# A streaming encoder step: factors of the norms spread by transposes, sums of the first norm taken from a token-major copy of x on ScalarE, first norm made beside the last units of an FFN

## The chip, the core and the metric

The kernel runs on one core of one Trainium2 chip. The core has TensorE (PE in the profile; PEld is its weight load), VectorE (DVE), ScalarE (ACT), GpSimd (POOL) and SyncE (SP), which issues most transfers; 16 DMA engines move the data. The metric is device time in microseconds (us). The kernel before takes 2417.05 us, the median of three runs (2413.43 to 2418.78).

## What is computed

One layer over 2048 prompt tokens and 8 x 16 sample tokens, width 1024, all in fp32. The layer normalizes x, projects it, runs four mixers side by side (a state-space scan, windowed attention, a short convolution, a convolution with layer norm), projects back, adds, and then runs a SwiGLU FFN of width 2816; a last norm ends it.

```python
def rms_norm(x, g):
    xf = x.astype(jnp.float32)
    y = xf * lax.rsqrt(jnp.mean(xf * xf, axis=-1, keepdims=True) + EPS)
    return (y * g.astype(jnp.float32)).astype(x.dtype)
...
    u = rms_norm(x, norm_mix) @ w_in
...
    mix = jnp.concatenate([ya, yb.astype(x.dtype), yc, yd], axis=-1)
    x = x + mix @ w_out
    hf = rms_norm(x, norm_ffn)
    x = x + (jax.nn.silu(hf @ w_gate) * (hf @ w_up)) @ w_down
...
    y_prompt = rms_norm(xp, norm_final)
    y_sample = rms_norm(xs, norm_final)
```

## The kernel before

**Tiling.** Everything is kept feature-major: 128 features on the partitions, tokens along the free axis, eight tiles deep for the width of 1024. The tokens are cut into five chunks c0 to c4 of 256, 512, 512, 512 and 384 tokens (c3 holds three prompt tiles and the 128 sample tokens). A matrix product is made in three passes: weights and activations are split into a high and a low part (`split`, `split_w`: a copy on ScalarE and a difference on VectorE), and `group` (L235) issues high x high (L239), high x low (L240) and low x high (L241) for each of the eight depth tiles. A unit, one weight tile of 128 output features, is 24 such matmuls.

**Weights.** `load_w` loads a raw tile (`fr`, two buffers) by SyncE's queue, ScalarE writes the high part (L204) and VectorE the low part (L184) into a `w` tile (three buffers). Some split tiles are stored to DRAM (`kept`) and loaded again for later chunks.

**Stages.** `weave` puts a list of units in order and runs steps of other work (tokens of generators) after given units. For c0 and c1 the program is: `proj_out(c)` (8 units), `proj_in(next)` (21 units, or what is left of them) with `norm2(c)` beside it, `ffn(c)` (44 gate and up units and 24 down units, the last six being the last gate, the last up and four downs that also square the result for the final norm) with the mixers of the next chunk beside it. c2 to c4 are woven differently: the FFN of c2 beside `proj_in` of c3 and c4, and the FFN of c3 and c4 together at the end, in an arithmetic of seven products (`quad`, L1129).

**The norms.** Each has three steps. Sums: squares on ScalarE, added up over the eight depth tiles on VectorE (`add_square`, into `ns`). Factors: `rstd_of` takes the sum over the partitions with one matmul by a column of ones per 128 tokens (L265), and `newton` makes the inverse root with ten small VectorE instructions. Spread: `spread` puts the factors of 128 tokens on all partitions by a matmul of the broadcast column with the identity (L272), into a PSUM tile `px`; then VectorE multiplies each depth tile by weight and factor and the tile is split into `act` tiles (16 buffers). `spread` serves the norm ahead of the mixers (`norm1`), the norm ahead of the FFN (`norm2`), the final norm and the end of two mixers (`end_ssd`, `end_conf`): 17 + 10 + 10 + 17 + 17 = 71 tiles of 128 tokens. The last two chunks use `spread_one` (L1046) for the norms behind their mixers.

**The first norm of c1 to c4** loads x twice by SyncE's queue: eight depth tiles for the sums (`norm1_stats`, L326) and eight for the scaling (`norm1`, L334), all through the three `nt` buffers. c0 keeps x in `act` tiles and is not touched by the change but for `spread`. The steps of `norm1(c2)` stand beside `proj_out(c1)` and those of `norm1(c3)` beside `proj_out(c2)` (L1000, L1006).

**Order.** A scheduler in the framework orders instructions by priority and by when it thinks that buffers come free. Weight loads have a higher priority. Each engine then runs its own list strictly in order, and SyncE's queue too; a matmul is bound to a place behind the last unit by `run` (L953).

Of the kernel before, what the change touches and what calls it, by code (L numbers as in the profile page):

```python
# [13 lines left out]
ALU = mybir.AluOpType  # L14
# [3 lines left out]
P = 128  # L18
# [97 lines left out]


@with_exitstack
def stream_step(ctx: ExitStack, tc: tile.TileContext, cfg, x, w_in, w_out, w_gu, w_down, tab, con, dist_p, dist_s,
                h0, xst, sst, gst, kc, vc, y, o_ssm_p, o_ssm_s, o_xc_p, o_xc_s, o_k_p, o_k_s, o_v_p, o_v_s,  # L120
                o_s_p, o_s_s, o_g_p, o_g_s):
    nc = tc.nc
# [20 lines left out]
    def mk(pool_, shape, tag, dt=F32, **kw):  # L143
        uid[0] += 1
        return pool_.tile(shape, dt, tag=tag, name=f"{tag}_{uid[0]}", **kw)
# [48 lines left out]
    def bc(a, shape):  # L194
        return a.to_broadcast(shape)
# [73 lines left out]
    def spread(r, T):  # L269
        pr = mk(px, [P, 512], "px")  # L270
        for b in range(T // P):
            pe.matmul(pr[:, b * P:(b + 1) * P], bc(r[:, b:b + 1], [P, P]), ident, start=True, stop=True)  # L272
        return pr[:, :T]

    def add_square(ss, src, T, first, eng=dve):
# [25 lines left out]

    def norm1_stats(c):
        T, o = c["T"], c["off"]
        ss = mk(np_, [P, TM], "ns", bufs=1)[:, :T]
        hold = c["i"] == 0 and KT * T <= 4 * TM
        if hold:

            c["x"] = []
            sq = []
            with tc.high_priority(offset=8 * AHEAD):  # L310
                xs = [mk(ap, [P, 2, KT // 4, T], "act") for _ in range(2)]
                for j in range(4):
                    sync.dma_start(xs[j // 2][:, j % 2], x[:, 2 * j:2 * j + 2, o:o + T])
                    c["x"] += [xs[j // 2][:, j % 2, k] for k in range(KT // 4)]
                qs = [mk(ap, [P, 2, KT // 4, T], "act") for _ in range(2)]
                for j in range(4):
                    sq.append(qs[j // 2][:, j % 2])
                    act.activation(sq[j], xs[j // 2][:, j % 2], AF.Square)
                for q in sq[1:]:
                    tt(sq[0], sq[0], q, ALU.add)  # L320
                tt(ss, sq[0][:, 0], sq[0][:, 1], ALU.add)
            yield
            c["r1"] = rstd_of(ss, T, D)
            yield
            return
        for k in range(KT):  # L326
            xt = mk(np_, [P, TM], "nt", bufs=B["nt"])[:, :T]
            sync.dma_start(xt, x[:, k, o:o + T])
            add_square(ss, xt, T, k == 0, dve)
        yield  # L330
        c["r1"] = rstd_of(ss, T, D)
        yield

    def norm1(c):  # L334
# [615 lines left out]
        yield  # L950


    def run(token):  # L953
        if tail[0] is None:
            next(token)
        else:
            with tc.issue_after(tail[0]):
                next(token)
# [12 lines left out]
    def twice(g, n=2):  # L971
        return [g] * n
# [14 lines left out]
    for t in twice(norm1_stats(chunks[0])) + twice(norm1(chunks[0]), 4):  # L987
# [5 lines left out]
    m0 = mixers(c0, True)  # L993
    nb0 = c0["blocks"]

    weave(units, (twice(norm1_stats(c1)) + twice(norm1(c1), 4), 6, n - 1), (m0[:nb0], 10, 22),
          (m0[nb0:], 18, len(units) - 1))
    for c, nxt, after in ((c0, c1, c2), (c1, c2, c3)):
        i = c["i"]
        weave(proj_out(c), *([(twice(final(chunks[i - 1]), 5), 0, 8), (twice(norm1(nxt), 4), 1, 8)] if i else []))  # L1000
        weave(proj_in(nxt, W_IN_TILES[0 if i else EARLY:]), (twice(norm2(c), 5), 0, 7))
        units = ffn(c)
        weave(units, (mixers(nxt), 0, int(len(units) * 0.85)),
              (twice(norm1_stats(after)), int(len(units) * 0.3), len(units) // 2))

    weave(proj_out(c2), (twice(final(c1), 5), 0, 8), (twice(norm1(c3), 4), 1, 8))  # L1006
    f = ffn(c2)
    def beside(c, s, units, end):

# [6 lines left out]

    s3 = proj_in(c3, SPREAD)
    units = s3[:5] + merge(s3[5:], f[:24]) + f[24:36]
    weave(units, (twice(norm2(c2), 5), 0, 5), *beside(c3, s3, units, len(units) - 1), (twice(norm1_stats(c4)), 20, 35))
    s4 = proj_in(c4, SPREAD)  # L1020
    units = proj_out(c3) + f[36:39] + merge(s4, f[39:44]) + f[44:53]
    weave(units, ([stats2(c3)], 8, 9), (twice(norm1(c4), 4), 8, 11), *beside(c4, s4, units, len(units) - 1))
# [260 lines left out]
def layout(cfg, inputs):  # L1283

    a = {k: np.asarray(v) for k, v in inputs.items()}
    f = np.float32

    def fm(t):

        return t.reshape(t.shape[0], -1, P).transpose(2, 1, 0)  # L1290

    xp, xs = a["x_prompt"][0], a["x_sample"].reshape(NS, D)
    parts, p0 = [], 0
    for i, n in enumerate(cfg.chunks):
        parts.append(xp[p0:p0 + n * P])
        p0 += n * P
        if i == cfg.sample_in:
            parts.append(xs)
    x = fm(np.concatenate(parts, 0))


    o = dict(z=0, x=256, B=512, C=640, dt=768, q=772, k=1028, v=1156, b=1284, c=1540, h=1796, a=2052, g=2308)
    hd = np.arange(64)

    def pair(base, t):
        return np.concatenate([base + HEADS[2 * t] * 64 + hd, base + HEADS[2 * t + 1] * 64 + hd])

    cols = []
    for n in W_IN_TILES:
        if n in ("z0", "z1", "x0", "x1", "q0", "q1"):  # L1310
            cols.append(pair(o[n[0]], int(n[1])))
        elif n == "dt":
            cols.append(o["dt"] + np.repeat(np.array(HEADS), 32))
        elif n in ("B", "C", "k", "v"):
            cols.append(o[n] + np.arange(P))
        else:
            cols.append(o[n[0]] + int(n[1]) * P + np.arange(P))
    w_in = a["w_in"][0][:, np.concatenate(cols)].reshape(KT, P, len(cols), P).transpose(2, 1, 0, 3)

    rows = np.concatenate([pair(0, 0), pair(0, 1), pair(256, 0), pair(256, 1), np.arange(512, 1024)])  # L1320
    w_out = a["w_out"][0][rows].reshape(KT, P, KT, P).transpose(2, 1, 0, 3)
    nff = cfg.nff
    w_gu = np.stack([a[n][0].reshape(KT, P, nff, P).transpose(2, 1, 0, 3) for n in ("w_gate", "w_up")], 1)
    w_down = a["w_down"][0].reshape(nff, P, KT, P).transpose(1, 2, 0, 3)

    tab = np.zeros((P, NTAB), f)

    def put(name, v, j=0):
        v = v.reshape(P, -1)
        tab[:, TAB[name] + j:TAB[name] + j + v.shape[1]] = v  # L1330

    for n, s in (("gmix", a["norm_mix"][0]), ("gffn", a["norm_ffn"][0]), ("gfin", a["norm_final"])):
        put(n, s.reshape(KT, P).T)
    inner = [pair(0, 0), pair(0, 1), 256 + np.arange(P), 384 + np.arange(P)]
    for j in range(4):
        put("xw", a["ssm_conv_w"][0][:, inner[j]].T, 4 * j)
        put("xb", a["ssm_conv_b"][0][inner[j]], j)
    for j in range(2):
        s = slice(j * P, (j + 1) * P)
        put("cw", a["cconv_w"][0][:, s].T, 31 * j)  # L1340
        put("sw", a["sconv_w"][0][:, s].T, 3 * j)
        put("cb", a["cconv_b"][0][s], j)
        put("lng", a["cconv_ln_g"][0][s], j)
        put("lnb", a["cconv_ln_b"][0][s], j)
        put("dsk", np.repeat(a["ssm_d"][0][[HEADS[2 * j], HEADS[2 * j + 1]]], 64), j)
        put("sng", a["ssm_norm"][0][pair(0, j)], j)
    put("dtb", np.repeat(a["ssm_dt_bias"][0][list(HEADS)], 32))
    put("alog", np.repeat(a["ssm_a_log"][0][list(HEADS)], 32))
    sinks = a["swa_sinks"][0]
    put("sinkp", np.tile(sinks[None], (P, 1)))  # L1350
    grp = (np.arange(P) // DEC_T) % 2
    for sg in range(2):
        for kv in range(2):
            put("sinks", sinks[kv * 2 + grp], sg * 2 + kv)

    con, bp, bs = constants()
    h0 = a["state_ssm"][0][:, list(HEADS)].transpose(3, 0, 1, 2).reshape(P, DEC_B, 256)
    xst = np.stack([a["state_ssm_conv"][0][:, :, inner[j]].transpose(2, 0, 1) for j in range(4)])
    sst = a["state_sconv"][0].reshape(DEC_B, 2, 2, P).transpose(2, 3, 0, 1)
    gst = a["state_cconv"][0].reshape(DEC_B, 30, 2, P).transpose(2, 3, 0, 1)  # L1360
    kc = a["cache_swa_k"][0].reshape(DEC_B, P, P).transpose(2, 0, 1)
    vc = a["cache_swa_v"][0].reshape(DEC_B, P, P).transpose(1, 0, 2)
    arrays = dict(x=x, w_in=w_in, w_out=w_out, w_gu=w_gu, w_down=w_down, tab=tab, con=con, dist_p=bp, dist_s=bs,
                  h0=h0, xst=xst, sst=sst, gst=gst, kc=kc, vc=vc)
    arrays = {k: np.ascontiguousarray(v) for k, v in arrays.items()}
    outs = dict(y=(P, KT, cfg.tokens), o_ssm_p=(P, 256), o_ssm_s=(P, DEC_B, 256), o_xc_p=(4, P, 3),
                o_xc_s=(4, P, DEC_B, 3), o_k_p=(P, P), o_k_s=(P, P), o_v_p=(P, P), o_v_s=(P, P), o_s_p=(2, P, 2),
                o_s_s=(2, P, DEC_B, 2), o_g_p=(2, P, 30), o_g_s=(2, P, DEC_B, 30))
    return arrays, outs
# [45 lines left out]
```

## Time and profile before

| what | value |
|---|---|
| median of 3 runs | 2417.05 us (2413.43, 2417.05, 2418.78) |
| the profiled execution: time | 2424.89 us |
| its span, first to last instruction | 2422.8 us |
| mean granted TensorE clock | 0.988 |
| instructions | 32494 |
| moved by DMA | 417.37 MB, mean 172 GB/s |

The span is one execution under the profiler, 2.1 us shorter than its own device time, and that execution is 7.8 us (0.3%) longer than the median of the runs. Rows of the page that begin with an engine's name give its busy time and share; rows with a line number give a group of equal instructions, with the mean of one and the time for which the engine stood idle just before them. "Idle" of an engine that nobody waits for is no loss. Rows of a timeline give start, length, engine, line, operation, and in brackets how long the engine had been idle and for whom.

### The profile page before, as it was taken

The page shows a single profiled execution, that of the slowest core. Times are in us where ns is not written, and L with a number is a line of the kernel's source. Part 1 is how long each engine was busy: PE and PEld are TensorE (multiplying, and loading weights), DVE is VectorE, ACT ScalarE, POOL GpSimd, SP SyncE. Part 2 cuts the span into 40 slices and gives each one's busy share as a digit, 9 for nine tenths or more (in the row PEclk, how much of TensorE's full clock was granted, in tenths as well). Part 3 has the DMA queues.
Part 4 walks back from the last instruction along what each step waited for, and adds up shares of the span by engine and source line. Part 5 has one row for each costly group of instructions (what it writes and reads, how often), then busy time and mean ns, then how long its engine had stood idle before and what let it go on. Part 6 is the DMA issues. An engine that isn't in the chain of part 4 may idle for free.

```text
span 2422.8 us, 32494 instructions
## 1 busy us (share of the span) xinstructions
PE 2358.7 (97%) x12451; PEld 2049.9 (85%) x12451; DVE 1597.3 (66%) x3001; ACT 880.8 (36%) x1466; POOL 144.2 (6%) x266
## 2 busy tenths in 40 slices
PE   6999999999999999998999999999999999999997
PEld 6888999988888888886878788888879999999997
DVE  7997998776884445567573554675687667663324
ACT  5544555433333333333312222233344444442221
POOL 0000000000000000001010000000001000000000
PEclk9999999999999999998999999999999999999998
DMA  6546444577555554465544336653633332339653
GB/s 213 202 160 226 149 153 161 165 260 270 192 176 174 174 174 167 173 240 147 176 146 145 143 123 225 209 168 116 213 109 135 113 131 95 119 122 319 211 182 119
DMA packets 133467, 417.37 MB, mean 172 GB/s; under 512 B 12880, under 2 KB 50672, under 8 KB 116160
## 3 DMA queue, kind: packets, MB, share of 16 engines
q1 hardware_dynamic: 115536, 324.57, 40.6%
q0 software_dynamic: 17776, 90.73, 9.8%
q8 instruction: 98, 1.61, 0.3%
q14 instruction: 57, 0.47, 0.1%
HBM read 324.07 MB, written 91.18 MB: 171 GB/s over the span
## 4 chain that ended last, share of the span: by engine, by line
PE 81%; issue 6%; DVE 6%; DMA 5%; ACT 2%; POOL 0%; SPq 0%; DVEq 0%; ACTq 0%; POOLq 0%
PE pm L239 17%; PE pm L240 17%; PE pm L241 17%; PE pm L1124 7%; PE pm L1125 7%; PE pm L1126 7%; DVE w L184 2%; PE px L1125 1%; PE px L1124 1%; PE px L1126 1%; DMA nt<-x 1%; ACT w L204 1%; DMA fr<-w_in 1%; DMA o_xc_s<-raw 1%; DVE mix L187 1%
## 5 line engine op out<-in xcount | busy, mean ns | idle before, releaser
L239 PE MATMUL pm<-act,w 128*128 128x512 f32 (+2 forms) x2216 | 803.8, 363 | 9.2 <-ACT act L199 7.4
L240 PE MATMUL pm<-act,w 128*128 128x512 f32 (+2 forms) x2216 | 794.6, 359 | 7.4 <-DVE act L184 7.3
L241 PE MATMUL pm<-act,w 128*128 128x512 f32 (+2 forms) x2216 | 795.5, 359 | 3.4 <-DVE w L184 3.4
L204 ACT ACTIVATE w<-fr 128x1024 fp32r<-128x1024 f32 (+2 forms) x380 | 393.6, 1036 | 893.4 <-PE pm L241 513.0
L184 DVE TENSOR_TENSOR w<-fr,w 128x1024 fp32r<-128x1024 f32 (+2 forms) x380 | 454.3, 1196 | 280.8 <-ACT w L204 279.1
L239 PEld LDWEIGHTS pm<-act,w 128*128 128x128 f32 x2216 | 418.9, 189 | 73.7 <-ACT act L199 9.2
L240 PEld LDWEIGHTS pm<-act,w 128*128 128x128 f32 x2216 | 419.5, 189 | 65.2 <-DVE act L184 8.7
L241 PEld LDWEIGHTS pm<-act,w 128*128 128x128 f32 x2216 | 419.1, 189 | 63.6 <-DVE w L184 4.7
L1124 PE MATMUL pm<-hf,w 128*128 128x448 f32 x616 | 225.2, 366 | 0.0
L1125 PE MATMUL pm<-hf,w 128*128 128x448 f32 x616 | 224.8, 365 | 0.0
L1126 PE MATMUL pm<-hf,w 128*128 128x448 f32 x616 | 223.8, 363 | 0.0
L187 DVE SCALAR_TENSOR_TENSOR mix<-raw,tabh,mix 128x384 f32<-128x384 f32 (+3 forms) x360 | 203.2, 593 | 2.4
L239 PE MATMUL pm<-h,w 128*128 128x512 f32 (+1 forms) x528 | 191.8, 364 | 5.3 <-ACT hf L199 3.3
L241 PE MATMUL pm<-h,w 128*128 128x512 f32 (+1 forms) x528 | 188.0, 357 | 0.0
L240 PE MATMUL pm<-h,w 128*128 128x512 f32 (+1 forms) x528 | 188.0, 357 | 0.0
L187 DVE SCALAR_TENSOR_TENSOR ft<-ft,pm 128x512 f32<-128x512 f32 (+1 forms) x132 | 78.6, 595 | 106.5 <-PE pm L241 90.5
L184 DVE TENSOR_TENSOR x<-x,pm 128x512 f32<-128x512 f32 (+2 forms) x184 | 108.2, 600 | 59.1 <-PE pm L241 51.2
L1126 PEld LDWEIGHTS pm<-hf,w 128*128 128x128 f32 x616 | 115.7, 188 | 9.4
L1124 PEld LDWEIGHTS pm<-hf,w 128*128 128x128 f32 x616 | 115.6, 188 | 9.4 <-ACT g L1138 0.3
L1125 PEld LDWEIGHTS pm<-hf,w 128*128 128x128 f32 x616 | 115.7, 188 | 8.3
L239 PEld LDWEIGHTS pm<-h,w 128*128 128x128 f32 x528 | 100.0, 190 | 23.6 <-ACT hf L199 3.7
L241 PEld LDWEIGHTS pm<-h,w 128*128 128x128 f32 x528 | 99.8, 189 | 15.2
(286 smaller groups left out, 2585.5 us busy)
## 6 DMA issues: line engine op xcount, KB each, us to landing
w<-kept SPq DMA_DIRECT2D x83, 1024.0 KB, 4.9
fr<-w_gu SPq DMA_DIRECT2D x154, 512.0 KB, 3.3
kept<-w POOLq DMA_DIRECT2D x51, 1024.0 KB, 6.3
fr<-w_down SPq DMA_DIRECT2D x84, 512.0 KB, 3.6
fr<-w_in SPq DMA_DIRECT2D x52, 512.0 KB, 4.0
fr<-w_out SPq DMA_DIRECT2D x40, 512.0 KB, 3.2
hm<-h POOLq DMA_DIRECT2D x44, 448.0 KB, 4.3
ht<-hm SPq DMA_DIRECT2D x40, 448.0 KB, 4.7
```

The lines of the kernel that those rows point to most:

```text
L184: return eng.tensor_tensor(out=out, in0=a, in1=b, op=op)
L187: return eng.scalar_tensor_tensor(out=out, in0=a, scalar=s, in1=b, op0=op0, op1=op1)
L204: act.activation(d[:, 0, :n], raw, AF.Copy)
L239: pe.matmul(ps[:, :T], wh, o[:, 0, :T], start=(i == 0), stop=False)
L240: pe.matmul(ps[:, :T], wh, o[:, 1, :T], start=False, stop=False)
L241: mm = pe.matmul(ps[:, :T], wl, o[:, 0, :T], start=False, stop=(i == n - 1))
L1124: pe.matmul(ps[:, :N], wh[:, i], a, start=first and i == 0, stop=False, skip_group_check=True)
L1125: pe.matmul(ps[:, :N], wh[:, i], b, start=False, stop=False, skip_group_check=True)
L1126: mm = pe.matmul(ps[:, :N], wl[:, i], a, start=False, stop=(i == n - 1), skip_group_check=True)
```

## The change

There are three edits. `spread` calls `pe.transpose` with the same operands where it called `pe.matmul`. `norm1_stats` for c1 to c4 reads rows of a second, token-major copy of x (`xr`, laid out on the host): for each 128 tokens two loads of 128 x 512, each squared on ScalarE in place with the sum of the row taken along (`accum_out`), and one VectorE addition of the two sums. The sums then stand with tokens on the partitions, as `newton` wants them, so the matmuls by ones and the adding up of eight tiles go. And the four steps of `norm1(c2)` and `norm1(c3)` now come beside the last six units of `ffn(c0)` and `ffn(c1)`; `norm1(c4)` stays where it was.

```diff
     def spread(r, T):
         pr = mk(px, [P, 512], "px")
         for b in range(T // P):
-            pe.matmul(pr[:, b * P:(b + 1) * P], bc(r[:, b:b + 1], [P, P]), ident, start=True, stop=True)
+            pe.transpose(pr[:, b * P:(b + 1) * P], bc(r[:, b:b + 1], [P, P]), ident)
         return pr[:, :T]
...
-        for k in range(KT):
-            xt = mk(np_, [P, TM], "nt", bufs=B["nt"])[:, :T]
-            sync.dma_start(xt, x[:, k, o:o + T])
-            add_square(ss, xt, T, k == 0, dve)
-        yield
-        c["r1"] = rstd_of(ss, T, D)
+
+        nb = T // P
+        sums = mk(cp, [P, 8], "n8", bufs=9)[:, :nb]
+        for b in range(nb):
+            for h in range(2):
+                xt = mk(np_, [P, TM], "nt", bufs=B["nt"])
+                part = mk(cp, [P, 1], "n1", bufs=4) if h else sums[:, b:b + 1]
+                sync.dma_start(xt, xr[o + b * P:o + (b + 1) * P, h * 512:(h + 1) * 512])
+                act.activation(xt, xt, AF.Square, accum_out=part)
+                if h:
+                    tt(sums[:, b:b + 1], sums[:, b:b + 1], part, ALU.add)
+            if b % 2:
+                yield
+        if nb % 2:
+            yield
+        v, r, t = (mk(cp, [P, 8], "n8", bufs=9)[:, :nb] for _ in range(3))
+        newton(v, r, t, sums, D)
+        c["r1"] = r
         yield
...
-        weave(proj_out(c), *([(twice(final(chunks[i - 1]), 5), 0, 8), (twice(norm1(nxt), 4), 1, 8)] if i else []))
+        weave(proj_out(c), *([(twice(final(chunks[i - 1]), 5), 0, 8)] if i else []))
...
-              (twice(norm1_stats(after)), int(len(units) * 0.3), len(units) // 2))
+              (stats1(after), int(len(units) * 0.3), len(units) // 2),
+              (twice(norm1(after), 4), len(units) - 6, len(units)))
...
-    weave(proj_out(c2), (twice(final(c1), 5), 0, 8), (twice(norm1(c3), 4), 1, 8))
+    weave(proj_out(c2), (twice(final(c1), 5), 0, 8))
```

**TensorE, the spread of c2's factors.** Before, it stands in `proj_out(c1)` behind that of the final norm of c0 (`px_5482`); `pm_5453` and `pm_5513` are units of `proj_out(c1)`.

```order
L240 MATMUL pm_5453<-act_4899,w_5450 128x512
L241 MATMUL pm_5453<-act_4899,w_5450 128x512
L272 MATMUL px_5482<-con_85,n_843_5431 128x128 x2
L272 MATMUL px_5489<-con_85,n_615_3821 128x128 x4
L239 MATMUL pm_5513<-act_2562,w_5510 128x512
```

Now it stands between the last gate unit (`pm_5180`) and the last up unit (`pm_5230`) of `ffn(c0)`.

```order
L240 MATMUL pm_5180<-act_2377,w_5177 128x256
L241 MATMUL pm_5180<-act_2377,w_5177 128x256
L272 MATMUL px_5208<-con_85,n_619_3889 128x128 x4
L239 MATMUL pm_5230<-act_2188,w_5227 128x256
L240 MATMUL pm_5230<-act_2188,w_5227 128x256
```

The spread has moved ahead by five units; it is one row of four blocks in both programs.

**VectorE, the end of `ffn(c0)`.** Before, from the product with the last gate (`ft` by `pm_5202`) to the first sums of the last downs (`x` by `pm_5269`, `pm_5282`); `w` are weight splits for the downs, `h_5261` is the low part of the last FFN tile.

```order
L187 SCALAR_TENSOR_TENSOR ft_5227<-ft_5227,pm_5202 128x256
L184 TENSOR_TENSOR w_5298<-fr_5296,w_5298 128x768
L187 SCALAR_TENSOR_TENSOR ft_5227<-ft_5227,pm_5235 128x256
L184 TENSOR_TENSOR w_5331<-fr_5329,w_5331 128x768
L184 TENSOR_TENSOR h_5261<-ft_5227,h_5261 128x256
L184 TENSOR_TENSOR x_302_1826<-x_302_1826,pm_5269 128x256
L184 TENSOR_TENSOR x_306_1860<-x_306_1860,pm_5282 128x256
```

Now, from the product with the last gate (`pm_5180`) to the first sum (`pm_5276`); `nt` and `act` are tiles of `norm1(c2)`, 512 tokens wide.

```order
L187 SCALAR_TENSOR_TENSOR ft_5205<-ft_5205,pm_5180 128x256
L187 SCALAR_TENSOR_TENSOR nt_5213<-nt_5213,tab_84,px_5208 128x512
L184 TENSOR_TENSOR w_5305<-fr_5303,w_5305 128x768
L184 TENSOR_TENSOR act_5216<-nt_5213,act_5216 128x512
L187 SCALAR_TENSOR_TENSOR nt_5219<-nt_5219,tab_84,px_5208 128x512
L187 SCALAR_TENSOR_TENSOR ft_5205<-ft_5205,pm_5230 128x256
L187 SCALAR_TENSOR_TENSOR nt_5259<-nt_5259,tab_84,px_5208 128x512
L184 TENSOR_TENSOR w_5350<-fr_5348,w_5350 128x768
L184 TENSOR_TENSOR act_5222<-nt_5219,act_5222 128x512
L184 TENSOR_TENSOR h_5256<-ft_5205,h_5256 128x256
L184 TENSOR_TENSOR act_5262<-nt_5259,act_5262 128x512
```

Three scalings and three splits of `norm1(c2)` have come among these rows, five of them ahead of the low part `h`.

**SyncE's queue at the start.** Before, from the fifth w_in tile (`fr_351`) to the seventh (`fr_440`); `nt` are tiles for the sums of c1, `x` the tiles of x that `proj_out(c0)` adds to.

```order
L222 DMA fr_351<-w_in 128x1024
L328 DMA nt_492<-x 128x512
L855 DMA x_331_2040<-x 128x256
L855 DMA x_336_2076<-x 128x256
L328 DMA nt_497<-x 128x512
L222 DMA fr_407<-w_in 128x1024
L222 DMA fr_440<-w_in 128x1024
```

Now, from the same fifth tile to the sixth (`fr_407`); `nt` by L333 are rows of the token-major copy, `nt` by L355 the first tiles of `norm1(c1)`.

```order
L222 DMA fr_351<-w_in 128x1024
L333 DMA nt_567<-xr 128x512
L333 DMA nt_570<-xr 128x512
L355 DMA nt_787<-x 128x512
L867 DMA x_307_1885<-x 128x256
L867 DMA x_312_1921<-x 128x256
L867 DMA x_317_1957<-x 128x256
L355 DMA nt_793<-x 128x512
L355 DMA nt_886<-x 128x512
L867 DMA x_322_1993<-x 128x256
L867 DMA x_327_2029<-x 128x256
L222 DMA fr_407<-w_in 128x1024
```

The sixth weight tile now has ten loads between it and the fifth instead of four.

More of the change, by code (lines that the diff above doesn't have):

```diff
@@ L118, in stream_step @@
 @with_exitstack
-def stream_step(ctx: ExitStack, tc: tile.TileContext, cfg, x, w_in, w_out, w_gu, w_down, tab, con, dist_p, dist_s,
+def stream_step(ctx: ExitStack, tc: tile.TileContext, cfg, x, xr, w_in, w_out, w_gu, w_down, tab, con, dist_p, dist_s,
                 h0, xst, sst, gst, kc, vc, y, o_ssm_p, o_ssm_s, o_xc_p, o_xc_s, o_k_p, o_k_s, o_v_p, o_v_s,
@@ L303, in norm1_stats @@
         T, o = c["T"], c["off"]
-        ss = mk(np_, [P, TM], "ns", bufs=1)[:, :T]
         hold = c["i"] == 0 and KT * T <= 4 * TM
         if hold:
+            ss = mk(np_, [P, TM], "ns", bufs=1)[:, :T]
             c["x"] = []
@@ L950, in final, with stats1 @@
         yield
+    def stats1(c):
+        g = norm1_stats(c)
+        return twice(g, (c["T"] // P + 1) // 2 + 1)
     def run(token):
@@ L994, in stream_step @@
     nb0 = c0["blocks"]
-    weave(units, (twice(norm1_stats(c1)) + twice(norm1(c1), 4), 6, n - 1), (m0[:nb0], 10, 22),
+    weave(units, (stats1(c1) + twice(norm1(c1), 4), 6, n - 1), (m0[:nb0], 10, 22),
           (m0[nb0:], 18, len(units) - 1))
@@ L1018, in stream_step @@
     units = s3[:5] + merge(s3[5:], f[:24]) + f[24:36]
-    weave(units, (twice(norm2(c2), 5), 0, 5), *beside(c3, s3, units, len(units) - 1), (twice(norm1_stats(c4)), 20, 35))
+    weave(units, (twice(norm2(c2), 5), 0, 5), *beside(c3, s3, units, len(units) - 1), (stats1(c4), 20, 35))
     s4 = proj_in(c4, SPREAD)
@@ L1298, in layout @@
             parts.append(xs)
-    x = fm(np.concatenate(parts, 0))
+    xr = np.concatenate(parts, 0)
+    x = fm(xr)
     o = dict(z=0, x=256, B=512, C=640, dt=768, q=772, k=1028, v=1156, b=1284, c=1540, h=1796, a=2052, g=2308)
@@ L1362, in layout @@
     vc = a["cache_swa_v"][0].reshape(DEC_B, P, P).transpose(1, 0, 2)
-    arrays = dict(x=x, w_in=w_in, w_out=w_out, w_gu=w_gu, w_down=w_down, tab=tab, con=con, dist_p=bp, dist_s=bs,
+    arrays = dict(x=x, xr=xr, w_in=w_in, w_out=w_out, w_gu=w_gu, w_down=w_down, tab=tab, con=con, dist_p=bp, dist_s=bs,
                   h0=h0, xst=xst, sst=sst, gst=gst, kc=kc, vc=vc)
```

## The prediction

> **What bounds the kernel now.** I began with the page: busy shares, then the 40 slices.
>
> ```profile
> PE 2358.7 (97%) x12451; PEld 2049.9 (85%) x12451; DVE 1597.3 (66%) x3001; ACT 880.8 (36%) x1466; POOL 144.2 (6%) x266
> ...
> PE   6999999999999999998999999999999999999997
> PEld 6888999988888888886878788888879999999997
> DVE  7997998776884445567573554675687667663324
> ```
>
> PE is busy in nearly every slice. VectorE comes near it only in the first quarter (slices 2 to 12: c0, the projections of c1, `ffn(c0)`). Busy matmul time alone could hide waits, so next I read who PE waits for.
>
> ```profile
> PE px L265 <- DVE ns L184: 12.4, 2, 10.8
> PE pm L239 <- ACT act L199: 7.4, 4, 3.9
> PE pm L240 <- DVE act L184: 7.3, 2, 6.0
> ```
>
> The waits of PE are few: 10.8 us of the first is the start of the kernel, and most of the other two is one place, around 1116 us, of which more below. So the kernel is bound by the matmuls that PE is given, and a matmul taken away anywhere but in those waits is time won. The opposite holds too: VectorE work that moves costs nothing until PE runs out of operands or of free accumulators.
>
> **The change, part by part.** *The spreads.* Groups by line and shape give the counts, and three stretches of PE's timeline the prices.
>
> ```profile
> L272 PE MATMUL px<-con,n 128*128 128x128 f32 x142 | 19.8, 282 | 4.2 <-DVE n L187 4.2
> L663 PE MATMUL px<-con,b 128*128 128x128 f32 x132 | 22.2, 280 | 3.8 <-ACT b L652 3.8
> L265 PE MATMUL px<-con,ns 128*128 128x1 f32 x88 | 11.2, 245 | 12.4 <-DVE ns L184 12.4
> ```
> ```profile
> 1080.93 0.39 PE L240 MATMUL pm<-act,w 128*128 128x512 f32 x1
> 1081.16 0.40 PE L241 MATMUL pm<-act,w 128*128 128x512 f32 x1
> 1081.40 1.05 PE L272 MATMUL px<-con,n 128*128 128x128 f32 x8
> 1082.21 0.48 PE L239 MATMUL pm<-act,w 128*128 128x512 f32 x1
> 1082.52 0.40 PE L240 MATMUL pm<-act,w 128*128 128x512 f32 x1
> ```
> ```profile
> 790.11 0.40 PE L241 MATMUL pm<-act,w 128*128 128x512 f32 x1
> 790.35 1.03 PE L663 MATMUL px<-con,b 128*128 128x128 f32 x8
> 791.14 0.48 PE L239 MATMUL pm<-act,w 128*128 128x512 f32 x1
> 791.45 0.39 PE L240 MATMUL pm<-act,w 128*128 128x512 f32 x1
> ```
>
> The code makes 71 spreads of 128 tokens, and the chip ran 142 instructions at L272: an fp32 matmul is two instructions. L663 is a transpose that the kernel has already, with the same identity and shape: the code makes four of them in each of 33 tiles, and the chip ran 132, one each. The price is what a group pushes back: from the L241 at 1081.16 to the second matmul behind the group, 1.36 us pass, of which two steps of 0.23 (1080.93 to 1081.16) are the matmuls' own; 0.90 is left for eight, 0.112 each. The transposes give 791.45 - 790.11 - 0.46 = 0.88 for eight, 0.110 each. One block so falls from 0.224 to 0.110, and 71 blocks give **-8.1 us**. All stand in PE's queue between matmuls, so no cover takes this away; bounds: -8.1 and 0 (if a broadcast operand were no cheaper as a transpose, the row of L272 itself).
>
> A page speaks of this price. The Trainium skill, "TensorE: Matmul & The Clock Gate", Terms, has a transpose mode that is four times faster for FP32; by that, taken as an estimate, the term would be 71 x 0.168 = 11.9 us. The rows here show half, not a quarter, and the rows decide.
>
> *The sums.* For c1 to c4 the matmuls by ones go: 15 blocks of 128 tokens, two instructions each, 30 of the 88 above.
>
> ```profile
> 1073.42 0.95 PE L265 MATMUL px<-con,ns 128*128 128x1 f32 x8
> 1074.23 0.52 PE L239 MATMUL pm<-act,w 128*128 128x512 f32 x1
> ```
>
> Eight take 0.81 us to the next matmul's start, as the eight spreads did (1081.40 to 1082.21), so 0.112 each: 30 x 0.112 = **-3.4 us**. What comes in their place is off PE:
>
> ```profile
> L184 DVE TENSOR_TENSOR ns<-ns,nt 128x512 f32<-128x512 f32 x56 | 38.7, 690 | 24.6 <-ACT nt L280 24.2
> L646 ACT ACTIVATION_READ_ACCUMULATOR b<-b,ng 128x1 f32 x68 | 12.7, 187 | 0.0
> L184 DVE TENSOR_TENSOR n<-n,n 128x4 f32<-128x4 f32 x30 | 4.8, 161 | 0.8
> L199 ACT ACTIVATE act<-nt 128x512 fp32r<-128x512 f32 x40 | 25.0, 629 | 48.8 <-DVE nt L187 48.5
> ```
> ```profile
> fr<-w_in SPq DMA_DIRECT2D x52, 512.0 KB, 4.0
> ```
>
> VectorE loses seven additions of 0.69 us per chunk of 512 and gains four of about 0.16: some 4.2 us less each for c1, c2 and c3, a little less for c4. ScalarE keeps as many squares and gains a read of the accumulator behind each, 30 x 0.187 = 5.6 us on an engine that is 36% busy; I cost it at nothing, and at most 5.6 if all of it stood on the path. The loads are as many bytes in as many or fewer pieces (eight of 256 KB; for c4 six in place of eight of 192 KB). The last two rows, a split of a norm tile on ScalarE and a weight load from issue to landing, are for what follows.
>
> *The start.* Only in the first chunk is VectorE's relief worth time.
>
> ```profile
> core 0: us, PE busy (x) PEld busy (x) DVE busy (x) ACT busy (x) POOL busy (x), PEclk, DMA share, GB/s
> ...
> 18.00:84.00 66.00, 60.98 (x478) 58.08 (x478) 58.70 (x136) 41.07 (x78) 2.12 (x5) 1.00 0.59 199
> ...
> 452.00:465.00 13.00, 12.32 (x104) 12.10 (x103) 9.69 (x19) 6.17 (x12) 0.00 (x0) 1.00 0.51 168
> 991.00:1019.00 28.00, 28.00 (x123) 22.78 (x122) 16.43 (x23) 10.38 (x15) 1.37 (x2) 1.00 0.53 188
> ...
> 1071.00:1122.00 51.00, 37.84 (x160) 30.22 (x161) 30.37 (x73) 11.21 (x22) 5.81 (x7) 0.87 0.41 123
> ```
>
> From 18 to 84 us PE lacks 5.0 us and VectorE is busy for 58.7 of 66; 4.2 us of its work goes. Against this, SyncE's queue now puts ten loads, some of which wait for squares on ScalarE, between the fifth and the sixth weight tile, where four stood. That tile must wait for its raw buffer in any case, and the squares that its forerunners wait for stand ahead of the weight split that frees it, so I expect it hardly later, with more transfers in flight beside it. Between the two I take **-1.5 us**; bounds -5.0 (all that PE lacks) and +4.0 (one weight load, landed late in full).
>
> *The moved norm.* Each of eight tiles costs VectorE a scaling and a split. Their pace in a row is seen in `norm2`:
>
> ```profile
> 1083.00 2.06 DVE L187 SCALAR_TENSOR_TENSOR nt<-x,tab,px 128x512 f32<-128x512 f32 x3
> 1084.98 1.89 DVE L184 TENSOR_TENSOR act<-nt,act 128x512 fp32r<-128x512 f32 x3
> ```
>
> That is 0.66 + 0.60 = 1.26 us a tile, 10.1 a chunk. It leaves `proj_out(c1)` and `proj_out(c2)`, where PE hardly waited; there the one thing won is this:
>
> ```profile
> 1072.14 0.50 PE L240 MATMUL pm<-act,w 128*128 128x512 f32 x1 [1.27 <-DVE act L184]
> ```
>
> PE stood for the last tile of `norm1(c3)`; made 50 us earlier, it will be there: **-1.3 us**. The work arrives at the ends of `ffn(c0)` and `ffn(c1)`. At the end of `ffn(c0)` units are half as wide and VectorE is free for only 13.00 - 9.69 = 3.3 us. By the order, six scalings and five splits (7.0 us) come ahead of the last sum that frees an accumulator there; 7.0 - 3.3 = 3.7 us too much. The four accumulators absorb some of it, at least the last few sums, which the next units don't wait for at once. I take **+2.5**, nearer to 3.7 than to nothing; bounds 0 and +10.1. What waits behind these rows is the low part `h` and the sums that free accumulators; on ScalarE the split of the first tile waits until the last up unit has read the `act` buffer that it takes over, and a weight split stands behind it. At the end of `ffn(c1)` VectorE has 28.00 - 16.43 = 11.6 us free for the 10.1: **+0.5**, bounds 0 and +5.
>
> SyncE's queue: three tiles of each moved norm are loaded long ahead and hold the three `nt` buffers through the FFN, where nobody else asks for them until its last downs; the other five stand between the w_out loads, which have a unit of 24 x 0.23 = 5.5 us each to land in. At no cost; if that cover fails, one load of 4.0 us.
>
> *What stays.* The largest hole after the start is this one:
>
> ```profile
> 1116.48 0.80 PE L240 MATMUL pm<-act,w 128*128 128x512 f32 x1 [6.00 <-DVE act L184]
> ```
>
> PE waits for `norm2(c2)`, whose last tiles stand on VectorE behind copies into `raw` buffers that wait for transfers. The order keeps them there (one tile more is now behind the first copy), so I leave these 12 us as they are, and neither win nor lose them.
>
> **Sum.** -8.1 - 3.4 - 1.5 - 1.3 + 2.5 + 0.5 = -11.3 us. Against the profiled execution, 2424.9 us (span 2422.8 and 2.1 around it), that is 2413.6; the median of the runs is 7.8 us lower, so I forecast 2417.05 - 11.3 = **2405.8 us**.
>
> **Rivals.** (a) *VectorE has room and the start gains all.* For it: the mean free time above, and four accumulators. Then the ends cost 0 and the start -5.0: -17.8, **2399.3**. (b) *The crowded ends cost more than the matmuls give*, slower than before. The mechanism: ScalarE's split of a norm tile waits for the last up unit, the weight splits behind it come late, and each norm tile stands on the path in full, with 0.63 on ScalarE and 1.26 on VectorE. At both ends that is 2 x 8 x 1.89 = 30.2 us, less 14.3 from the other terms: +16, **2433**. It decides from the point at which the two ends together cost over 14.3 us. Against it: the weights of the first two downs stand ahead of that split, and 7.0 us of VectorE work is all that the order puts ahead. (c) *The transposes save nothing*, since a broadcast column is run as two instructions or at twice the price: -8.1 goes, -3.2 is left, **2413.9**. Against it stands L663 alone, whose operand is a full tile. (d) *The clock.* A TensorE that looks idle is slowed: in 1071 to 1122, with the 12 us hole, the granted clock is 0.87, 6.6 us of 51. If each of the some 20 groups of transposes had that effect, it would cost 132 us less 11.3: **2538**. Against it, the stretch 452 to 465 has full clock, and the matmul steps behind the eight transposes at 790 are those behind the eight matmuls at 1081. The Trainium skill, "TensorE: Matmul & The Clock Gate", Part 4: PE-mode transpose, says that transposes do not count as busy for the clock; by that rule (d) would happen where transposes fill a whole window, and the eight in a row here did not show it.
>
> **How the numbers follow.** Forecast 0.60, (a) 0.20, (b) 0.10, (c) 0.07, (d) 0.03. A change of less than 0.2% (4.8 us) cannot be told from none here. Of the forecast 0.56 is faster and 0.04 within 0.2%; (a) is all faster; (b) is 0.07 slower and 0.03 within; (c) is 0.03 faster and 0.04 within; (d) is slower. Sum: faster 0.79, same 0.11, slower 0.10. The range for 8 in 10 runs from a little below (a), 2396, to where (b) would begin, 2417: it leaves out (d), most of (b) and a tail of (a).
>
> **What would show it.** L272 runs 71 times and eight-block groups push PE back by 0.45; L265 runs 30 times fewer for `ns`. The gap at 1072 is gone and the one at 1116 is not. Between the last up unit of `ffn(c0)` and the first unit of `proj_out(c1)`, PE takes about 2.5 us more than now. Wrong would be: PE waiting for `w` or `h` over 5 us at either end; weight loads in the first 60 us landing later than now; or two instructions per transpose.

## The result, and the profile after

The change makes the kernel slower. Run side by side, the kernel before takes 2417.91 us (median of 4 runs, 2413.43 to 2426.26) and the changed one 2439.16 us (4 runs, 2437.12 to 2444.45): ratio 1.0088, 95% interval 1.0069 to 1.0106. The forecast was 2405.8.

| | before | after |
|---|---|---|
| profiled execution | 2424.89 us | 2439.48 us |
| its span | 2422.8 us | 2437.7 us |
| mean granted clock | 0.988 | 0.988 |
| TensorE standing, gaps over 0.3 us summed | 55.4 us | 55.2 us |

The page of after, busy time by engine and the slices that were shown of before:

```profile
PE 2373.2 (97%) x12350; PEld 2036.4 (84%) x12350; DVE 1584.0 (65%) x2988; ACT 882.3 (36%) x1494; POOL 146.9 (6%) x266
...
PE   6999999999999999997999999999999999999997
PEld 6788999887877778886877788988879999999997
DVE  7897998855784446656573454675687667663324
```

TensorE has 101 instructions less, 71 + 30 as forecast, and is busy 14.5 us *longer*. It does not wait more, and the clock is the same. The groups by line and shape of after show that the instructions went where they should:

```profile
L272 PE MATMUL px<-con,n 128*128 128x128 f32 x71 | 11.6, 279 | 3.5 <-DVE n L187 3.4
L265 PE MATMUL px<-con,ns 128*128 128x1 f32 x58 | 7.6, 248 | 11.8 <-DVE ns L184 11.8
L334 ACT ACTIVATION_READ_ACCUMULATOR nt<-nt 128x1 f32 x30 | 5.6, 186 | 0.0
```

So the time must lie in the matmuls that stay. The next two fences are stretches of the trace, first of before and then of after; the columns are start and end, length, TensorE's busy time with the number of its matmuls, granted clock, DMA share and GB/s. In the first stretch only 512-column matmuls run, in the two others only the last stage's 448-column ones.

```profile
568.00:638.00 70.00, 70.00 (x308) 1.00 0.64 226
1870.00:2050.00 180.00, 180.00 (x892) 1.00 0.34 116
2210.00:2360.00 150.00, 150.00 (x752) 1.00 0.70 229
```
```profile
568.00:638.00 70.00, 70.00 (x302) 1.00 0.61 222
1870.00:2050.00 180.00, 180.00 (x885) 1.00 0.35 118
2210.00:2360.00 150.00, 150.00 (x743) 1.00 0.74 240
```

TensorE is busy all the time in both, at full clock, and gets fewer matmuls done, even in the last stage, which the diff does not touch. The time from one matmul's start to the next, summed over the whole trace by width, gives the bill:

```
columns  steps   median before, after   sum before, after (us)
512      5160    229   233 ns           1223.7  1240.9   +17.2
448      2899    202   204 ns            584.7   589.9    +5.2
384       686    173   176.5 ns          120.9   121.9    +1.0
256      2238    118   114 ns            276.5   279.6    +3.1
```

That is +26.5 us (the sums hold some waits and stretches at half clock too; the 256-column median fell). Less 101 instructions of 0.112 us, 11.3, it gives +15.2; the spans differ by 14.9. In this bill the pace costs over twice what the instructions that are gone were worth. How much of that worth was really won is a question for the experiments.

### The profile page after: what moved, and what is told of

It is laid out like the page before. It is cut to its first block, busy times and chain, and to the rows that moved or that the text cites. A ratio compares the mean times of both kernels' runs of the same rounds, so it can differ in the third digit from the quotient of the medians.

```text
span 2437.7 us, 32296 instructions
## 1 busy us (share of the span) xinstructions
PE 2373.2 (97%) x12350; PEld 2036.4 (84%) x12350; DVE 1584.0 (65%) x2988; ACT 882.3 (36%) x1494; POOL 146.9 (6%) x266
## 3 DMA queue, kind: packets, MB, share of 16 engines
q8 instruction: 97, 1.59, 0.3%
## 4 chain that ended last, share of the span: by engine, by line
PE 52%; DMA 2%; DVE 1%; ACT 0%; issue 0%; DVEq 0%; POOL 0%; ACTq 0%; POOLq 0%
PE pm L239 8%; PE pm L240 8%; PE pm L241 8%; PE pm L1141 7%; PE pm L1143 7%; PE pm L1142 7%; PE px L1143 1%; PE px L1141 1%; PE px L1142 1%; DMA o_xc_s<-raw 1%; DVE x L187 0%; DMA act<-kc 0%; DMA raw<-xst 0%; PE px L675 0%; DMA w<-kept 0%; PE px L703 0%
## 5 line engine op out<-in xcount | busy, mean ns | idle before, releaser
L241 PE MATMUL pm<-act,w 128*128 128x512 f32 (+2 forms) x2216 | 800.0, 361 | 2.3 <-DVE w L184 2.2
L240 PEld LDWEIGHTS pm<-act,w 128*128 128x128 f32 x2216 | 419.9, 190 | 73.8 <-DVE act L184 11.5
L241 PEld LDWEIGHTS pm<-act,w 128*128 128x128 f32 x2216 | 419.6, 189 | 66.9 <-DVE w L184 3.3
L239 PE MATMUL pm<-h,w 128*128 128x512 f32 (+1 forms) x528 | 193.9, 368 | 7.3 <-ACT hf L199 3.3
L240 PE MATMUL pm<-h,w 128*128 128x512 f32 (+1 forms) x528 | 190.7, 362 | 0.1
L241 PE MATMUL pm<-h,w 128*128 128x512 f32 (+1 forms) x528 | 190.6, 362 | 0.0
```

Source lines behind the costliest of these rows:

```text
L239: pe.matmul(ps[:, :T], wh, o[:, 0, :T], start=(i == 0), stop=False)
L240: pe.matmul(ps[:, :T], wh, o[:, 1, :T], start=False, stop=False)
L241: mm = pe.matmul(ps[:, :T], wl, o[:, 0, :T], start=False, stop=(i == n - 1))
```

## Experiments

Where each tile lies in a partition's memory stands in the built program. The change adds a tag of four one-column tiles, `n1`, 32 bytes each with padding, in the pool that lies below the weights. So the weights `w` move from 29600 to 29728 bytes, while their partners in the matmul, `act` and `h`, stay where they were. That was the first theory; the rivals were that transposes, order or loads slow TensorE. In what follows every ratio is to the kernel before, run in the same set.

### Addresses alone, and the change without them

The first kernel (e1) is the one before with two lines more. The second (e2) is the changed kernel, with the second half's sums put into columns that the first half's tile does not use:

```
+    pad = mk(cp, [P, 32], "pad")
+    pool.memset(pad, 0.0)
```
```
-                part = mk(cp, [P, 1], "n1", bufs=4) if h else sums[:, b:b + 1]
+                part = s8[:, 4 + b:5 + b] if h else sums[:, b:b + 1]
```

> The kernel before with one unused tile of 128 bytes per partition in the pool that lies below the weights; nothing else is changed. Address theory (the four new one-column tiles of the change, 32 bytes each, move the weights by 128 bytes, and TensorE takes 233 in place of 229 ns from one 512-column matmul to the next): the steps become 233 ns here too, and the time is 20 to 32 us above the kernel before, 2437 to 2449. Rival (the transposes, the new order or the loads slow the matmuls): no change, within 3 us.

> The changed kernel, with the second half's sums in columns 4 to 7 of the tile that holds the first half's, so that the four new tiles go and every tile lies where it lay before the change. Address theory: steps of 229 ns again, and the time that the prediction's terms give, 2406 with 2399 to 2413 as bounds. Rival (the change itself slows the matmuls): steps of 233 ns and 2436 to 2442.

Measured: 128 unused bytes cost 2449.46 beside 2426.32 us, ratio **1.0088** (1.0073 to 1.0102), as much as the whole change. The changed kernel at the old addresses takes 2422.66 us, ratio **0.9982** (0.9973 to 0.9992). The same stretches, of the padded kernel and then of the changed one at the old addresses:

```profile
568.00:638.00 70.00, 70.00 (x302) 1.00 0.61 220
1870.00:2050.00 180.00, 180.00 (x885) 1.00 0.36 121
2210.00:2360.00 150.00, 150.00 (x744) 1.00 0.72 242
```
```profile
568.00:638.00 70.00, 70.00 (x307) 1.00 0.67 237
1870.00:2050.00 180.00, 180.00 (x892) 1.00 0.35 116
2210.00:2360.00 150.00, 150.00 (x752) 1.00 0.70 233
```

Both kernels whose weights were moved by 128 bytes have 302 in the first stretch, both others 307 or 308. Over the whole trace the median step at 512 columns is 233 ns in the changed kernel and in e1, and 229 ns in before, in e2 and in the five kernels further below that keep the old addresses (e3, e5, e6, e7, e12). In e1's trace TensorE, VectorE, ScalarE and SyncE's queue also run the same lists in the same order as before. So for the slowdown the rivals fall: in e1 transposes, order and loads are those of before, and the slowdown is there. The expectation for the second kernel was half right: it is faster, but by 4.4 us, not by 11.

### A map of addresses

> Leaves out the whole computation: it runs groups of 24 matmuls, as the kernel's units are made, with nothing beside them, for 512, 448 and 256 columns, with the weights' address moved in steps of 32 bytes over 512 and with the moving operand's address moved likewise, and the weights alone on to 2048 bytes. Address theory: the step between matmuls depends on the two addresses; for weights at 416 and operands at 480 (modulo 512) it is about 229 ns at 512 columns, for 32 and 480 about 233. Rival: one step for all addresses, within 1 ns.

The mean step in ns, by the distance of the two operands (address of the moving operand less that of the weights, modulo 256 bytes); median over 31 to 33 groups of 24 matmuls for each cell, worked out from the start times in the trace, the 384-column line from a later run of 96 matmuls a cell:

```
distance      0      32     64     96     128    160    192    224
512 columns   226.7  233.4  229.3  233.4  233.5  233.9  233.4  233.1
448 columns   206.7  204.5  200.0  205.3  204.4  200.5  202.1  204.3
384 columns   173.6  173.3  173.3  176.7  176.0  173.5  174.7  173.5
256 columns   119.6  117.9  117.8  120.1  118.4  117.3  117.8  118.3
```

Of 768 groups all but 23 lie within 1 ns of the median of their distance, whatever the addresses themselves, and the medians stay when the weights move on by whole multiples of 256 bytes, up to 1792: of these two addresses, the distance alone counts. It holds with no other engine at work. Before, `w` lies at 160 and `act` and `h` at 224 modulo 256: distance 64, 229.3. After, `w` lies at 32: distance 192, 233.4. In the last stretch above, the 448-column operand `ht` lies at 224 too: 150 us over 752 and 743 matmuls are 199.5 and 201.9 ns, where the map has 200.0 at distance 64 and 202.1 at 192. The fall of the 256-column median to 114 ns is not in these medians (117.8 at both distances). By the map, 512 columns do best at distance 0, and 448 columns worst of all there and best at 64.

### The best addresses

The next kernel (e8) takes that at its word. It has unused tiles of 64 bytes ahead of the weights (now at 224: distance 0 in the stages of 512 columns) and of 64 or 192 bytes ahead of the last stage's operands (now at 32: distance 64).

```
+    pool.memset(mk(cp, [P, 16], "pad"), 0.0)
...
+    pool.memset(mk(p1, [P, 16], "pad1"), 0.0)
     xp = ctx.enter_context(tc.tile_pool(name="xp"...
...
+    pool.memset(mk(p2, [P, 48], "pad2"), 0.0)
     late["xq"] = later.enter_context(...
...
+    pool.memset(mk(p3, [P, 48], "pad3"), 0.0)
```

> The changed kernel without the four new tiles, with unused tiles that put the weights at 224 modulo 256, the distance 0 from act and h, and the last stage's operands at 32 modulo 256, the distance 64. Address theory by the map: 512-column steps of 226.7 in place of 229 (5160 of them, 11.9 us less), 256-column ones of 119.6 in place of 118 (3.8 us more), 448-column ones 200 in place of 202 (2 us less): 10 us below the changed kernel at the old addresses, ratio to before 0.994. Rival (only what was seen between 229 and 233 holds in the kernel, where other engines use the memory too): 0.998.

> The kernel before, unchanged but for the unused tiles that set the best addresses. Address theory: 12 us less by the 512-column matmuls, 2 less and 4 more by the others: 10 us, ratio 0.996, and with the kernel that has also the new sums and transposes in the same set of runs it shows what these are worth at equal addresses. Rival (the gain at the best addresses came from the change): 1.000.

Measured: **0.9933** (0.9913 to 0.9953), 2407.28 beside 2423.03 us, for the changed kernel; **0.9953** (0.9940 to 0.9965), 2411.77 beside 2422.78 us, for the kernel before with the same unused tiles. The stretches of the changed kernel at the best addresses:

```profile
568.00:638.00 70.00, 70.00 (x310) 1.00 0.61 221
1870.00:2050.00 180.00, 179.71 (x898) 1.00 0.35 119
2210.00:2360.00 150.00, 150.00 (x751) 1.00 0.64 200
```

310 where 302 and 308 stood: the median 512-column step is 227 ns, in the other kernel at these addresses too. The map holds inside the kernel, in both directions; this version beats both kernels. What the change itself is worth at the best addresses, 0.9933 against 0.9953, looks like what it is worth at the old ones, 0.9982 against 1, but the two come from different sets of runs and their intervals overlap, so it is not clear of noise there.

### Why only 4 us were left of 11

Three kernels take the changed one at the old addresses (e2) apart, and two put transposes alone into the kernel before.

```
e3:  before, with   pe.transpose(pr[:, b * P:(b + 1) * P], bc(r[:, b:b + 1], [P, P]), ident)
e5:  changed, with  pe.matmul(pr[:, b * P:(b + 1) * P], bc(...), ident, start=True, stop=True)
e6:  changed, with  (twice(norm1(nxt), 4), 1, 8)  beside proj_out(c1) and proj_out(c2) again
e7:  changed, with  norm1_stats as before
e12: before, with every transpose issued twice
```

> The kernel before with the spreads made by transposes and nothing else changed; addresses as before. The prediction's first term: 71 instructions less at this line, 8.1 us less (ratio 0.9966). Rival that a transpose of a broadcast column saves nothing: ratio 1.000. Rival that transposes lower the clock or the pace behind them: ratio above 1.003 and steps above 229 ns.

> The changed kernel at the addresses of before, with the spreads as matmuls again; the new sums and the moved norm stay. Prediction's term: 8.1 us above the changed kernel at these addresses (ratio 0.998), so about 1.0015. Theory that the transposes give part of it back through the clock (TensorE is granted half its clock for 3.4 us at a time, and kernels with transposes showed more such stretches): the mean granted clock is back at 0.989 from 0.988, no such stretch shows at 70 to 90 us, and the ratio is 1.000 to 1.001. Rival (the clock has nothing to do with the transposes): the clock stays at 0.988 and the stretch at 73 us is there.

> The changed kernel at the addresses of before, with the first norms of c2 and c3 beside proj_out again; transposes and new sums stay. Prediction's terms for the move: +2.5 and +0.5 at the two FFN ends, -1.3 at proj_in of c3, so 1.7 us less without it (ratio 0.9975). Theory from the trace (the end of ffn of c0 costs 4.8 us more, 1.7 of it by the clock): 3 to 5 us less, ratio 0.9965, and the gaps at 436 to 466 us are gone while the one at 1072 is back. Rival (the move is worth its gap): ratio 0.9985 or more.

> The changed kernel at the addresses of before, with the first norm's sums made as before (squares of x added up on VectorE, matmuls by ones); transposes and the moved norm stay. Prediction's terms: 3.4 us for 30 matmuls and 1.5 at the start are lost, ratio 1.000. Theory from the trace (the start did not gain but is 4.6 us longer, 3.4 of it by the clock, with transposes in it): the matmuls' 3.4 us alone, ratio 0.9995, and the start stays as late as with the new sums. Rival (the new sums' loads make the start late): the start is 4 us earlier, ratio 0.998.

| kernel | ratio (95%) | mean clock of its runs, of before's |
|---|---|---|
| transposes alone (e3) | 1.0008 (0.9992 to 1.0024) | 0.9869, 0.9891 |
| changed, old addresses (e2) | 0.9982 (0.9973 to 0.9992) | 0.9880, 0.9891 |
| without transposes (e5) | 0.9993 (0.9981 to 1.0005) | 0.9892, 0.9893 |
| norm not moved (e6) | 0.9971 (0.9958 to 0.9984) | 0.9886, 0.9893 |
| old sums (e7) | 1.0002 (0.9988 to 1.0016) | 0.9878, 0.9893 |

Against e2, the new sums are worth 0.0020 (4.8 us; 4.9 forecast) and the move costs 0.0011 (2.7 us; 1.7 forecast). Each difference has some 0.0016 of uncertainty, and e2 ran in another set than the last three, so only that of the sums is, just, clear of noise. In the trace of e6 the gap ahead of `proj_in` of c3 is back, with 1.66 us, and of the five gaps of e2 at the end of `ffn(c0)` the three last are gone. The transposes are worth 0.0011 there (not clear of noise either; e5 was expected at 1.0000 to 1.0015 and is a little faster, with the clock and the start as its theory had them) and nothing by themselves, where 8.1 us were forecast. Yet TensorE does spend 8 us less on them, as the timeline of after shows around one group of four:

```profile
1087.82 0.40 PE L240 MATMUL pm<-act,w 128*128 128x512 f32 x1
1088.06 0.40 PE L241 MATMUL pm<-act,w 128*128 128x512 f32 x1
1088.29 0.60 PE L272 MATMUL px<-con,n 128*128 128x128 f32 x4
1088.65 0.48 PE L239 MATMUL pm<-act,w 128*128 128x512 f32 x1
1088.96 0.39 PE L240 MATMUL pm<-act,w 128*128 128x512 f32 x1
```

From the L241 at 1088.06 to the second matmul behind the group are 0.90 us, of which 0.47 are two steps: 0.43 for four blocks, where before took 0.90 for its eight instructions. So what became of it? In the trace of the kernel with the transposes alone, TensorE is busy 9.2 us less (2349.5 in place of 2358.7), and it stands for 63.2 us where before stands for 55.4: 7.8 us more. Two stretches, of before, and of the kernel with transposes alone:

```profile
0.00:95.00 95.00, 74.11 (x571) 1.00 0.61 204
1060.00:1145.00 85.00, 71.71 (x301) 0.90 0.55 167
```
```profile
0.00:95.00 95.00, 70.73 (x524) 0.96 0.62 200
1060.00:1145.00 85.00, 68.56 (x291) 0.90 0.50 162
```

In the start and around the hole at 1116 TensorE is busy 3.4 and 3.2 us less in the same time. And in the start the clock is 0.96 in place of 1.00: two stretches of 3.41 us at half clock, at 80 and 87 us, which before does not have. The kernels with 71 transposes have such stretches between 73 and 88 us in six profiles of seven, those without transposes in none of four, and in the clock column above the four with transposes are all a little lower than before. In e3 the difference, 0.0022 of 2420 us, is by estimate 5.3 us of work at full speed. Is it the transposes that the clock does not like, or the waits that they leave? Two runs ask.

> Leaves out the whole computation: dense 512-column matmuls on TensorE, with stretches of 500 transposes, of 250 fp32 matmuls of the same shape, of groups of 8 transposes after every 24 dense matmuls, and of 4 fp32 matmuls after every 24. Theory that transposes count as idle for the clock: in the stretch of 500 transposes, about 55 us, the granted clock falls to 0.5 and it takes twice the time, in the stretch of 250 fp32 matmuls it stays at 1.0; in the mixed stretches it stays at 1.0 in both, or falls for the transposes alone. Rival (the clock falls with waits alone): 1.0 everywhere. Beside it the steps at 384 and 128 columns for eight distances of the two addresses: the map's theory is that they too depend on the distance.

> The kernel before with every spread made by transposes, and each transpose issued twice into the same place: 142 instructions at this line as before, 0.110 us each, so TensorE's time for the spreads is that of before, but all of it in transposes. Theory that what the transposes save turns into waits, and waits trip the clock: nothing is saved, nothing is tripped, ratio 1.000, clock 0.989, no half-clock stretch at 70 to 90 us. Rival that transposes themselves count as idle for the clock: twice as many of them, clock 0.987 or less, ratio 1.002 to 1.005, and the stretch at 70 to 90 us is there.

The first, in stretches of its trace (the last columns as above, with weight loads, ScalarE and GpSimd between): dense matmuls, 500 transposes, 250 fp32 matmuls of the same shape, and groups of 8 transposes between dense matmuls.

```profile
9.00:120.00 111.00, 110.83 (x477) 91.57 (x478) 7.68 (x9) 0.00 (x0) 1.00 0.00 1
121.00:175.00 54.00, 54.00 (x497) 54.00 (x496) 0.00 (x0) 0.00 (x0) 1.00 0.01 1
...
285.00:340.00 55.00, 55.00 (x495) 55.00 (x495) 0.00 (x0) 0.00 (x0) 1.00 0.00 1
...
455.00:700.00 245.00, 245.00 (x1236) 205.91 (x1235) 0.00 (x0) 0.00 (x0) 1.00 0.00 1
```

Full clock everywhere: 500 transposes in a row did not lower it. The second has as many transposes again and gives TensorE back its 8 us: ratio 0.9999 (0.9984 to 1.0015), mean clock 0.9904 beside 0.9905, and in the trace's two stretches neither the half clock at the start nor the lower busy time at the hole:

```profile
0.00:95.00 95.00, 72.55 (x562) 1.00 0.61 201
1060.00:1145.00 85.00, 72.02 (x311) 0.92 0.54 171
```

So the transposes as such are harmless. But the two kernels differ in one thing more: the scheduler orders instructions by when it expects buffers to come free, and with 71 instructions less on TensorE it chose another order. Two stretches of SyncE's queue, of before and of the kernel with the transposes alone, show one place:

```profile
81.16 0.33 SPq L343 DMA_DIRECT2D nt<-x  x1
84.38 0.33 SPq L222 DMA_DIRECT2D fr<-w_in  x1
84.98 3.63 SPq L343 DMA_DIRECT2D nt<-x  x2
```
```profile
84.92 1.26 SPq L343 DMA_DIRECT2D nt<-x  x2
86.98 0.33 SPq L222 DMA_DIRECT2D fr<-w_in  x1
```

A weight load now stands behind one norm tile more. The trace of e3 has seven such places in SyncE's queue, and more in the lists of VectorE, ScalarE and TensorE; that of e12 has none in SyncE's queue or TensorE's list and a handful in the others. So e12 gave back both TensorE's time and, nearly, the order of before. Whether the saving is lost to waits that any shorter queue would meet, or to the order that came with it, these runs do not tell apart. The first alone does not explain the start: there e3 is 4.9 us *later* than before at the 500th matmul, 3.4 of it by the two stretches at half clock, and a wait that only takes back what was saved would leave it level.

Nor is it shown what sets off the half-clock stretches. Without the one at the very end, e3's trace has 41.0 us of them and before's 40.9, at 63.2 and 55.4 us of standing, so more standing does not simply mean more half clock.

### The move at the best addresses

The last kernel has the best addresses and the norms beside `proj_out`, as e6.

> Transposes and new sums, the first norms left beside proj_out, and the best addresses of the map: weights at 224, last stage's operands at 32 modulo 256. Address theory and the measured price of the move add up: 0.9971 (not moved) less 0.0049 (what the addresses gave the changed kernel) is 0.992, some 19 us below the kernel before. Rival (either gain is noise of one set of runs): 0.995 or more.

Measured: 0.9941 (0.9923 to 0.9959), between the two expectations and no better than the 0.9933 with the move. Its mean clock was 0.9873, the lowest but one of all kernels. Whether the move costs anything at these addresses stays open.

## Why the prediction was wrong

- **The sum** has no term for the pace of the matmuls that stay. It took "two steps of 0.23" as "the matmuls' own" on both sides of the change. They are 229 and 233 ns at 512 columns (202 and 204 at 448), because the diff line that allocates `n1` moves the weights by 128 bytes. That is the step that failed; by itself it costs 0.88%, 21 us (e1). With the 0.18% that the rest wins (e2) that makes 0.70%, at the lower end of the interval measured for the whole, 0.69 to 1.06%. The profile of before could not have priced it: it shows nearly one distance only.
- **The spreads, -8.1.** The price was right, 0.43 us for four blocks. What failed is "a matmul taken away anywhere but in those waits is time won". The runs showed in its place that TensorE stands 7.8 us longer, mostly in the start and around the hole at 1116, and has a lower clock over all runs (e3). By itself the step won nothing that could be measured; in the changed kernel 2.7 us of it may be left, with as much uncertainty. With the instruction count and, nearly, the order of before (e12) neither shows; which of the two decides stays open.
- **The sums, -3.4, and the start, -1.5.** Together 4.8 us by e7, right in size, though in the profiles the start is not where they show: up to the 500th matmul e2 is 4.6 us *later* than before, 3.4 of it half clock, with the old sums (e7) 3.5 later, and without transposes (e5) 2.6 earlier. The sixth weight tile is issued at 29.54 us in the changed kernel and at 29.26 in before: hardly later, as foreseen.
- **The gap before `proj_in` of c3, -1.3.** It is gone. The next hole, in the timeline of the changed kernel at the old addresses:

```profile
1112.94 0.79 PE L240 MATMUL pm<-act,w 128*128 128x512 f32 x1 [4.11 <-DVE act L184]
1121.42 0.80 PE L240 MATMUL pm<-act,w 128*128 128x512 f32 x1 [6.37 <-DVE act L184]
1126.68 0.80 PE L239 MATMUL pm<-act,w 128*128 128x512 f32 x1 [3.61 <-ACT act L199]
```

  These are 14.1 us, where before stood for 2.10 + 6.00 + 3.92 = 12.0. But the hole is not the same from one kernel to the next: 12.2 us in the changed kernel itself, 13.4 in e6, where the norm is not moved. That the gap's 1.3 us came back here is not shown. "I leave these 12 us as they are" was right of what ends the hole, and right of its length in the changed kernel.
- **The end of `ffn(c0)`, +2.5.** Between the 2500th and the 3000th matmul e2 takes 4.8 us more than before, 1.7 of it half clock, and with the norm not moved (e6) 0.1 less. The mechanism was the named one: the five waits there are for VectorE, four of them for the sums that free accumulators. The first two stand in e6 as well, with 1.59 and 0.64 us, so the move's own are the last three, 1.7 us:

```profile
441.00 0.39 PE L239 MATMUL pm<-h,w 128*128 128x256 f32 x1 [1.61 <-DVE ft L187]
442.96 0.55 PE L239 MATMUL pm<-h,w 128*128 128x256 f32 x1 [0.63 <-DVE x L184]
...
465.52 0.38 PE L239 MATMUL pm<-h,w 128*128 128x256 f32 x1 [0.38 <-DVE x L184]
467.53 0.38 PE L239 MATMUL pm<-h,w 128*128 128x256 f32 x1 [0.68 <-DVE x L184]
469.46 0.36 PE L239 MATMUL pm<-h,w 128*128 128x256 f32 x1 [0.61 <-DVE x L184]
```

- **The end of `ffn(c1)`, +0.5.** Nothing to be seen: e2 is 0.6 and 0.8 us earlier in the two stretches of 500 matmuls around it.
- **The rivals.** (b) gave a time near the measured one, 2433, by a mechanism that did not happen: TensorE stands 4.0 us in place of 2.0 between 430 and 470, not 15. (c) foresaw the size of the transposes' gain for a wrong reason: each is one instruction at half the price. (d), the clock, was wrong in how it would fall, since 500 transposes in a row keep it; a little lower it was, 0.9880 beside 0.9891 at the old addresses (e2). No rival had the addresses.

## What to carry to other kernels

Where TensorE is busy 97% of the time, compare the step from matmul to matmul before anything else: if it has changed in code that the diff does not touch, look at where the tiles lie, since one new 32-byte tile moves all that is allocated behind it, and test with an unused tile of the same size. To judge any edit to such a kernel, hold the operands' addresses fixed, or what is measured is the addresses too. An instruction taken from a busy engine need not be worth its time: here 9.2 us less of TensorE's work, by itself, won nothing. Where a scheduler sets the order by the times it expects, an edit of one line also changes the order on other engines; compare the lists before and after, and do not read such an experiment as one change alone.

## What the runs showed of the hardware

- With fp32r operands the step between 512-column matmuls runs from 226.7 to 233.9 ns, and between 448-column ones from 200.0 to 206.7, by the distance of the two operands' addresses modulo 256 bytes, with nothing else at work (e4). Why it is so, these runs do not show.
- In the kernels' traces the clock falls to one half in stretches of 3.41 us and multiples (3.41, 6.83, 10.24 and so on; only the last one, at the end of the trace, has other lengths), and one can begin as a wait shorter than that ends: at 73.8 us in e2, with a wait of 1.8 us. The Trainium skill, "TensorE: Matmul & The Clock Gate", Part 1, gives the window as 3413 ns, which agrees.
- 500 transposes of 128 x 128 fp32 take 0.109 us each, 250 fp32 matmuls of that shape 0.223 (two instructions of 0.112), all at full clock. The Trainium skill, "TensorE: Matmul & The Clock Gate", Part 4: PE-mode transpose, says that full clock doesn't engage for transposes; for 54 us of them, after dense matmuls, it did not fall here.
